# Narrow fp32 products of an RWKV-7 layer: one at a time, or four at a time in column groups

## The chip, the cores and the metric

The kernel runs on one core of one Trainium2 chip. The metric is the device time in microseconds of one execution. Times are the median of several executions; one further execution was taken with the hardware profiler, and all rows below come from that one.

## The reference

The program is a trunk of two layers over 512 frames of width 1024, batch 1. Layer 0 mixes time with RWKV-7, layer 1 with a convolution module; each is followed by cross-attention to 256 memory tokens and by a gated MLP. The change lies in the RWKV-7 mixer:

```
xr, xw, xk, xv, xa, xg = (h + xx * mu[i] for i in range(6))    # xx: the frame before, minus this one
r = xr @ w_r;  k = xk @ w_k;  v = xv @ w_v                      # 1024 x 1024 each
g = sigmoid(xg @ g1) @ g2                                       # g1: 1024 x 160
...
bonus = sum(rh * kh * r_k, axis=-1, keepdims=True) * vh         # one sum per head and frame, 16 heads of 64
out = ((y + bonus) * g) @ w_o
```

Two of its products have few output rows: the last 32 of the 160 columns of `g1`, and the bonus sums, of which there are 16 for each frame.

## The kernel before

Everything is held transposed, with features on the 128 partitions and the 512 frames in the free dimension, so the width of 1024 is 8 tiles of 128 x 512. TensorE multiplies a stationary block of weights (128 rows by up to 128 columns) with a moving tile of 128 x 512 and adds up in PSUM, over the 8 tiles. There are two kinds of product. The large ones split weights and activations into a high and a low part in the fp32r format and make three products of them (L181 to L183). The small ones take plain fp32 operands: the trace shows each of them as two matmul records and two weight loads.

*Gate stage* (`rwkv`, L388 to L400). For each of the 8 tiles, `mix(5, i, ...)` (L366) makes the mixed input on ScalarE and VectorE in one of eight `xh` buffers. A 128-column product with `g1a` (L393) and a 32-column product with `g1b` (L394, written to PSUM partitions 0 to 31) follow at once, so the two shapes alternate. Their sums go through a sigmoid (L399) and are parked in DRAM until the end of the mixer.

*k, r and v stages.* For each of the three, `mixes` (L402) makes 8 split inputs, and `gemm_cols` (L205) multiplies: output tiles 0 and 1 go side by side, one input tile after the other, then tiles 2 to 7, with `wsplit` splitting each block of weights. A callback takes each output tile: `k_done` (some 25 small operations on ScalarE and VectorE), `r_done`, `v_done`. `r_done(p)` (L574) makes one scratch tile `rk` and sums it over each head by a 16-column product (L585) that accumulates over all eight p in one PSUM tile held for the whole stage; after p = 7 the sums are split into rows 0 to 15 and 32 to 47 of `self.rows` (L587 to L590), which are read in the chain after v.

Between these products run substitution steps (`subst_a`, `subst_b`, called at fixed steps from L425). `subst_a(1)` starts after r tile 4: TensorE products (L609), then on VectorE a long chain of dependent operations (L618 to L633) that lasts through the start of the v stage.

The order on each engine is not written by hand here. A planner orders the instructions before the run, by priorities (mostly program order, some lowered by `lower`) and by its own estimate of when operands are ready. Each engine then works in that order and waits where an operand is late. Scratch tiles with the tag `tmp` rotate over six buffers (`NTMP`, L135), PSUM tiles over three `g`, three `h` and two `kv` banks (L139).

Of the kernel before, what the change touches and what calls it, by code (L numbers as in the profile page):

```python
# [11 lines left out]
ALU = mybir.AluOpType  # L12
# [5 lines left out]
KT = D // 128  # L18
NP = 8
# [91 lines left out]
class Builder:  # L111
# [212 lines left out]
    def rwkv(self):  # L324
        nc, a = self.nc, self.a
        with ExitStack() as cx:
# [27 lines left out]
            h = self.x  # L354
# [7 lines left out]
            for i in range(KT):  # L362
                nc.vector.scalar_tensor_tensor(out=h[:, i, :], in0=h[:, i, :], scalar=self.vec("g_mix0", i),
                                               in1=rs, op0=ALU.mult, op1=ALU.mult)

            def mix(m, i, tag="mf", bufs=2):  # L366
                mf = self.t(self.gp, [128, T], tag, bufs=bufs)
                nc.scalar.activation(mf, h[:, i, :], AF.Copy, scale=cpr[:, (5 + m) * KT + i : (5 + m) * KT + i + 1])
                nc.vector.scalar_tensor_tensor(out=mf[:, 1:], in0=h[:, i, : T - 1], scalar=self.vec(f"mu{m}", i),
                                               in1=mf[:, 1:], op0=ALU.mult, op1=ALU.add)  # L370
                return mf
# [3 lines left out]
            ps = self.ps()  # L375
            for i in range(KT):
                for m, w, o in ((1, w1, 0), (4, a1, 64)):
                    nc.tensor.matmul(ps[o : o + 64, :], w[:, i * 64 : (i + 1) * 64], mix(m, i, "xh", KT),
                                     start=i == 0, stop=i == KT - 1)
# [8 lines left out]
            g1a = self.wraw(a["g1a"], KT * 128)  # L388
            g1b = self.wraw(a["g1b"], KT * 32)
            ps, ps2 = self.ps(), self.ps()  # L390
            for i in range(KT):
                mf = mix(5, i, "xh", KT)
                nc.tensor.matmul(ps, g1a[:, i * 128 : (i + 1) * 128], mf, start=i == 0, stop=i == KT - 1)  # L393
                nc.tensor.matmul(ps2[:32, :], g1b[:, i * 32 : (i + 1) * 32], mf, start=i == 0, stop=i == KT - 1)  # L394
            self.gpark = self.t(self.dp, [160, T], "gpark")
            for r0, q in ((0, ps), (128, ps2[:32, :])):
                n = q.shape[0]
                sg = self.tmp()
                nc.scalar.activation(sg[:n], q, AF.Sigmoid)  # L399
                nc.sync.dma_start(self.gpark[r0 : r0 + n], sg[:n])  # L400
# [51 lines left out]
            for w, m, done in (("w_k", 2, k_done), ("w_r", 0, r_done),  # L452
                               ("w_v", 3, v_done)):
                srcs = [a[w][p] for p in range(NP)]
                lead = self.lead(srcs)
                self.gemm_cols(srcs, mixes(m), done, lead)
# [17 lines left out]
            for i in range(KT):  # L474
                nc.sync.dma_start(self.x[:, i, :], a["xT"][i])
            self.gemm_cols(wo, og, self.addx, lead)

    def rowbcast(self, half, p, s, tag):

        ps = self.ps(tag).rearrange("p (a t) -> p a t", a=2)  # L480
        for j in range(2):
            self.nc.tensor.matmul(ps[:, j], self.selb[half][:, (p + j) * 128 : (p + j + 1) * 128], self.rows[:, s],
                                  start=True, stop=True)
        return ps
# [89 lines left out]
    def r_done(self, p, psr):  # L574
        nc = self.nc
        r = self.AR[:, 1, p, :]
        rk = self.tmp()
        nc.vector.tensor_tensor(out=r, in0=psr, in1=r, op=ALU.mult)
        as3 = lambda x_: x_.rearrange("p (c t) -> p c t", t=C)
        for h in range(2):  # L580
            rows = slice(64 * h, 64 * h + 64)
            nc.vector.tensor_tensor(out=as3(rk)[rows], in0=as3(r)[rows], in1=self.bk[p][rows, :, 1 - h, :], op=ALU.mult)
        if p == 0:
            self.bonps = self.ps("h")
        nc.tensor.matmul(self.bonps[0:16, :], self.ws[:, p * 16 : (p + 1) * 16], rk, start=p == 0, stop=p == NP - 1)  # L585
        if p == NP - 1:
            b = self.rows = self.t(self.r1, [128, T], "zw", F32R)  # L587
            nc.vector.memset(b.bitcast(F32), 0.0)
            nc.scalar.copy(b[0:16], self.bonps[0:16, :])
            nc.vector.tensor_tensor(out=b[32:48], in0=self.bonps[0:16, :], in1=b[0:16], op=ALU.subtract)  # L590

    def bkt(self, p, h, c):
        return self.bk[p][64 * h : 64 * h + 64, c, :, :].rearrange("p b t -> p (b t)")
# [893 lines left out]
```

## Time and profile before

| what | value |
|---|---|
| time, median of 3 runs | 1658.86 us (1658.69 to 1660.44) |
| profiled execution, its own time | 1656.06 us |
| span in that execution, first to last instruction | 1654.3 us |
| TensorE matmul busy | 1613.1 us, 98% of the span |
| VectorE busy | 1106.0 us, 67% |
| ScalarE busy | 794.8 us, 48% |
| mean granted TensorE clock | 0.996 |

The profiled execution's time holds 1.8 us that lie outside the span. Busy shares are means over stages that differ; the rows further down look at the stages one by one. PE is TensorE, DVE VectorE, ACT ScalarE, and L394 is line 394 of the kernel.

### The profile page before, as it was taken

The page shows a single profiled execution, that of the slowest core. Times are in us where ns is not written, and L with a number is a line of the kernel's source. Part 1 is how long each engine was busy: PE and PEld are TensorE (multiplying, and loading weights), DVE is VectorE, ACT ScalarE, POOL GpSimd, SP SyncE. Part 2 cuts the span into 40 slices and gives each one's busy share as a digit, 9 for nine tenths or more (in the row PEclk, how much of TensorE's full clock was granted, in tenths as well). Part 3 has the DMA queues.
Part 4 walks back from the last instruction along what each step waited for, and adds up shares of the span by engine and source line. Part 5 has one row for each costly group of instructions (what it writes and reads, how often), then busy time and mean ns, then how long its engine had stood idle before and what let it go on. Part 6 is the DMA issues. An engine that isn't in the chain of part 4 may idle for free. (4 is left out here: it accounts for less than half of the span.)

```text
span 1654.3 us, 24232 instructions
## 1 busy us (share of the span) xinstructions
PE 1613.1 (98%) x9742; PEld 1293.5 (78%) x9742; DVE 1106.0 (67%) x1795; ACT 794.8 (48%) x1242; POOL 73.1 (4%) x101
## 2 busy tenths in 40 slices
PE   7999989899999999999999999999999999999998
PEld 6575558898888888888888777767888888888887
DVE  4779976568766667777732479877766677777323
ACT  5876635766454344434422366645533434444222
POOL 0000000000000000000000024430000000000000
PEclk9999999999999999999999999999999999999999
DMA  6333322103441233332333331223412333323332
GB/s 237 114 99 109 105 65 90 53 22 115 135 140 51 86 120 94 98 103 90 96 95 94 112 107 51 65 89 103 140 52 89 91 98 94 102 92 93 97 95 83
DMA packets 55151, 159.77 MB, mean 97 GB/s; under 512 B 6144, under 2 KB 10368, under 8 KB 55040
## 3 DMA queue, kind: packets, MB, share of 16 engines
q1 hardware_dynamic: 55040, 158.24, 30.8%
q8 instruction: 76, 1.25, 0.3%
q14 instruction: 35, 0.29, 0.1%
HBM read 150.55 MB, written 7.67 MB: 96 GB/s over the span
## 5 line engine op out<-in xcount | busy, mean ns | idle before, releaser
L176 ACT CAST wh<-raw 128x1024 fp32r<-128x1024 f32 (+1 forms) x227 | 235.1, 1037 | 503.4 <-PE g L182 396.2
L182 PE MATMUL g<-xl,wh 128*128 128x512 f32 x1152 | 451.0, 392 | 4.1 <-DVE xl L177 3.6
L181 PE MATMUL g<-xh,wh 128*128 128x512 f32 x1152 | 452.9, 394 | 0.7 <-ACT xh L176 0.7
L183 PE MATMUL g<-xh,wl 128*128 128x512 f32 x1152 | 451.0, 391 | 2.5 <-DVE wl L177 2.5
L177 DVE TENSOR_TENSOR wl<-raw,wh 128x1024 fp32r<-128x1024 f32 (+1 forms) x227 | 274.7, 1210 | 164.2 <-ACT wh L176 163.8
L182 PEld LDWEIGHTS g<-xl,wh 128*128 128x128 f32 x1152 | 216.9, 188 | 54.0 <-DVE xl L177 6.6
L183 PEld LDWEIGHTS g<-xh,wl 128*128 128x128 f32 x1152 | 216.9, 188 | 50.4 <-DVE wl L177 3.3
L181 PEld LDWEIGHTS g<-xh,wh 128*128 128x128 f32 x1152 | 216.9, 188 | 48.4 <-issue 1.8
L181 PE MATMUL g<-ah,wh 128*128 128x512 f32 (+1 forms) x374 | 141.0, 377 | 0.0
L183 PE MATMUL g<-ah,wl 128*128 128x512 f32 (+1 forms) x374 | 140.9, 377 | 0.0
L182 PE MATMUL g<-al,wh 128*128 128x512 f32 (+1 forms) x374 | 140.9, 377 | 0.0
L1157 DVE TENSOR_TENSOR z<-g,rs 128x512 f32<-128x512 f32 x88 | 60.4, 688 | 70.8 <-PE g L183 69.2
L181 PEld LDWEIGHTS g<-ah,wh 128*128 128x128 f32 x374 | 70.4, 188 | 13.0
L182 PEld LDWEIGHTS g<-al,wh 128*128 128x128 f32 x374 | 70.4, 188 | 12.9
L183 PEld LDWEIGHTS g<-ah,wl 128*128 128x128 f32 x374 | 70.4, 188 | 12.7
L1277 POOL TENSOR_TENSOR dg<-i,wsp 128x256 fp32r<-128x256 f32 x70 | 48.2, 721 | 657.3 <-DVE wsp L1231 573.0
L176 ACT CAST ah<-tmp 128x512 fp32r<-128x512 f32 x44 | 27.3, 622 | 100.9 <-DVE z L1156 95.8
L1299 DVE SCALAR_TENSOR_TENSOR h<-u,cdw,h 128x512 f32<-128x512 f32 x98 | 73.8, 753 | 2.3
L321 DVE TENSOR_TENSOR x<-x,g 128x512 f32<-128x512 f32 x39 | 26.8, 688 | 68.7 <-PE g L183 68.7
L1162 DVE SCALAR_TENSOR_TENSOR tmp<-z,fdw,tmp 128x512 f32<-128x512 f32 x88 | 66.0, 752 | 2.9
L1161 DVE SCALAR_TENSOR_TENSOR tmp<-z,fdw,tmp 128x512 f32<-128x512 f32 x88 | 65.5, 746 | 0.4 <-ACT tmp L1160 0.4
L1160 ACT ACTIVATE tmp<-z,fdw 128x512 f32<-128x512 f32 x88 | 63.2, 720 | 4.7 <-DVE z L1157 1.5
(351 smaller groups left out, 2445.4 us busy)
## 6 DMA issues: line engine op xcount, KB each, us to landing
raw<-wi SPq DMA_DIRECT2D x84, 512.0 KB, 3.5
raw<-wo SPq DMA_DIRECT2D x33, 512.0 KB, 3.5
raw<-wv SPq DMA_DIRECT2D x16, 512.0 KB, 3.6
raw<-cwi SPq DMA_DIRECT2D x14, 512.0 KB, 3.6
raw<-wq SPq DMA_DIRECT2D x12, 512.0 KB, 4.4
raw<-wxo SPq DMA_DIRECT2D x12, 512.0 KB, 3.5
raw<-wo SPq DMA_DIRECT2D x16, 384.0 KB, 3.1
raw<-wk SPq DMA_DIRECT2D x10, 512.0 KB, 3.8
```

Source lines behind the costliest of these rows:

```text
L176: self.nc.scalar.copy(h, src)
L177: self.nc.vector.tensor_tensor(out=l, in0=src, in1=h, op=ALU.subtract)
L181: mm(out, lh, rh, start=start, stop=False)
L182: mm(out, lh, rl, start=False, stop=False)
L183: mm(out, ll, rh, start=False, stop=stop)
L321: self.nc.vector.tensor_tensor(out=self.x[:, n, :], in0=self.x[:, n, :], in1=ps, op=ALU.add)
L1157: nc.vector.tensor_tensor(out=z[:, 2:], in0=ps, in1=rs(), op=ALU.mult)
L1160: nc.scalar.activation(y, z[:, 2:], AF.Copy, scale=cw(2))
L1161: nc.vector.scalar_tensor_tensor(out=y, in0=z[:, 1 : T + 1], scalar=cw(1), in1=y, op0=ALU.mult, op1=ALU.add)
L1162: nc.vector.scalar_tensor_tensor(out=y, in0=z[:, 0:T], scalar=cw(0), in1=y, op0=ALU.mult, op1=ALU.add)
L1277: nc.gpsimd.tensor_tensor(out=dg[:, h], in0=i2.unsqueeze(1).unsqueeze(1).to_broadcast([128, 2, 2, 64]), in1=wsp[:, :, i, h, 2 * g : 2 * g ...
L1299: nc.vector.scalar_tensor_tensor(out=ac, in0=u[:, jt : jt + T], scalar=cw(jt), in1=ac if n else ln["c"], op0=ALU.mult, op1=ALU.add if n el ...
```

## The change

In the gate stage the 32-column products wait until four mixed inputs are there. Then four of them are issued one after the other, each with its own block of weights, its own input and its own 32 partitions of one PSUM tile. This happens twice, and the second four accumulate on the first. The new `groupsum` then copies partitions 32 to 63 to a scratch tile on ScalarE and adds the other three quarters on VectorE.

For the bonus sums, `r_done` keeps the `rk` tiles of four steps. At p = 3 and p = 7 it issues four 16-column products into the four quarters of a fresh PSUM tile. The first tile goes through `groupsum` at p = 3, the four quarters of the second are added at p = 7, and then the sums are split as before.

```diff
             ps, ps2 = self.ps(), self.ps()
+            mfs = []
             for i in range(KT):
                 mf = mix(5, i, "xh", KT)
                 nc.tensor.matmul(ps, g1a[:, i * 128 : (i + 1) * 128], mf, start=i == 0, stop=i == KT - 1)
-                nc.tensor.matmul(ps2[:32, :], g1b[:, i * 32 : (i + 1) * 32], mf, start=i == 0, stop=i == KT - 1)
+                mfs.append(mf)
+                if i % 4 == 3:
+                    for j in range(4):
+                        k = i - 3 + j
+                        nc.tensor.matmul(ps2[32 * j : 32 * j + 32, :], g1b[:, k * 32 : (k + 1) * 32], mfs[k],
+                                         start=i == 3, stop=i == KT - 1)
...
-            for r0, q in ((0, ps), (128, ps2[:32, :])):
+            for r0, q in ((0, ps), (128, self.groupsum(ps2, 32))):
...
+    def groupsum(self, ps, rows):
+
+        nc = self.nc
+        s = self.tmp()[:rows]
+        nc.scalar.copy(s, ps[32 : 32 + rows])
+        for j in (0, 2, 3):
+            nc.vector.tensor_tensor(out=s, in0=ps[32 * j : 32 * j + rows], in1=s, op=ALU.add)
+        return s
...
-        if p == 0:
-            self.bonps = self.ps("h")
-        nc.tensor.matmul(self.bonps[0:16, :], self.ws[:, p * 16 : (p + 1) * 16], rk, start=p == 0, stop=p == NP - 1)
+        if p % 4 == 0:
+            self.rks = []
+        self.rks.append(rk)
+        if p % 4 == 3:
+            ps = self.ps("h")
+            for j in range(4):
+                k = p - 3 + j
+                nc.tensor.matmul(ps[32 * j : 32 * j + 16, :], self.ws[:, k * 16 : (k + 1) * 16], self.rks[j],
+                                 start=True, stop=True)
+            if p == 3:
+                self.brow = self.groupsum(ps, 16)
         if p == NP - 1:
+            s = self.brow
+            for j in range(4):
+                nc.vector.tensor_tensor(out=s, in0=ps[32 * j : 32 * j + 16], in1=s, op=ALU.add)
             b = self.rows = self.t(self.r1, [128, T], "zw", F32R)
             nc.vector.memset(b.bitcast(F32), 0.0)
-            nc.scalar.copy(b[0:16], self.bonps[0:16, :])
-            nc.vector.tensor_tensor(out=b[32:48], in0=self.bonps[0:16, :], in1=b[0:16], op=ALU.subtract)
+            nc.scalar.copy(b[0:16], s)
+            nc.vector.tensor_tensor(out=b[32:48], in0=s, in1=b[0:16], op=ALU.subtract)
```

## Rows read from the trace of the kernel before

**Rows 1.** The page's busy time by engine.
```profile
PE 1613.1 (98%) x9742; PEld 1293.5 (78%) x9742; DVE 1106.0 (67%) x1795; ACT 794.8 (48%) x1242; POOL 73.1 (4%) x101
```
**Rows 2.** Windows: stretch, length, busy and instructions per engine, PE clock, DMA share, GB/s.
```profile
47.98:64.12 16.14, 16.14 (x33) 3.37 (x31) 11.99 (x17) 13.89 (x21) 0.00 (x0) 1.00 0.38 130
64.12:75.16 11.04, 11.04 (x50) 9.12 (x50) 7.46 (x10) 7.21 (x13) 0.00 (x0) 1.00 0.58 174
...
206.00:224.20 18.20, 16.46 (x303) 11.67 (x303) 10.44 (x15) 5.00 (x10) 0.00 (x0) 1.00 0.20 60
224.20:256.80 32.60, 27.82 (x110) 18.99 (x109) 31.91 (x71) 13.54 (x19) 0.00 (x0) 1.00 0.23 67
```
**Rows 3.** Timeline of PE, gate stage: start, duration, line, tile, count [idle before].
```profile
50.96 1.04 PE L394 MATMUL g<-xh,raw 128*32 128x512 f32 x2
51.93 1.12 PE L393 MATMUL g<-xh,raw 128*128 128x512 f32 x2
```
**Rows 4.** Timeline of PE, one plain 128-column product among split products.
```profile
184.14 1.02 PE L1043 MATMUL kv<-raw,tt 128*128 128x512 f32 x2
184.76 0.63 PE L181 MATMUL g<-xh,wh 128*128 128x512 f32 x1
185.23 0.39 PE L182 MATMUL g<-xl,wh 128*128 128x512 f32 x1
```
**Rows 5.** Timeline of PE, one bonus product among split products.
```profile
208.28 0.39 PE L182 MATMUL g<-xl,wh 128*128 128x512 f32 x1
208.60 1.03 PE L585 MATMUL h<-tmp,wsc 128*16 128x512 f32 x2
209.56 0.50 PE L183 MATMUL g<-xh,wl 128*128 128x512 f32 x1
209.89 0.39 PE L181 MATMUL g<-xh,wh 128*128 128x512 f32 x1
```
**Rows 6.** Timeline of PE, two 64-column products in two column groups (L378).
```profile
39.88 1.08 PE L378 MATMUL g<-xh,raw 128*64 128x512 f32 x4
40.88 0.70 PE L987 MATMUL kv<-tt 128*128 128x256 f32 x2
```
**Rows 7.** Timeline of DVE, gate stage.
```profile
53.15 1.41 DVE L369 SCALAR_TENSOR_TENSOR xh<-x,vecs,xh 128x511 f32<-128x511 f32 x2
...
64.50 0.75 DVE L369 SCALAR_TENSOR_TENSOR mf<-x,vecs,mf 128x511 f32<-128x511 f32 x1 [2.38 <-ACT mf L368]
...
68.39 1.36 DVE L177 TENSOR_TENSOR xl<-mf,xh 128x512 fp32r<-128x512 f32 x2
```
**Rows 8.** Timeline of ACT, gate stage.
```profile
61.34 1.28 ACT L399 ACT_TABLE_LOAD   x1
63.26 0.60 ACT L399 ACTIVATE tmp<-g 128x512 f32<-128x512 f32 x1 [0.63 <-PE g L393]
```
**Rows 9.** Timeline of DVE, r stage and start of v.
```profile
212.16 0.69 DVE L578 TENSOR_TENSOR AR<-g,AR 128x512 f32<-128x512 f32 x1 [3.91 <-PE g L183]
...
244.23 0.68 DVE L590 TENSOR_TENSOR zw<-h,zw 16x512 fp32r<-16x512 f32 x1
...
256.13 0.69 DVE L177 TENSOR_TENSOR xl<-mf,xh 128x512 fp32r<-128x512 f32 x1
```
**Rows 10.** Waits in 198.8 to 256.9: engine, line, releaser: us, times, longest.
```profile
PE h L585 <- DVE tmp L582: 1.7, 3, 0.7
```
**Rows 11.** Timeline of PE, start of the v stage.
```profile
246.01 0.50 PE L182 MATMUL g<-xl,wh 128*128 128x512 f32 x1 [2.62 <-DVE xl L177]
```
**Rows 12.** Windows of PE alone: stretch, length, busy, clock, DMA share, GB/s.
```profile
239.70:252.30 12.60, 8.55 (x32) 1.00 0.17 48
252.30:256.80 4.50, 4.50 (x21) 1.00 0.45 120
190.30:192.80 2.50, 0.02 (x1) 0.50 0.55 198
192.80:197.20 4.40, 4.40 (x11) 0.51 0.69 205
```

## The prediction

> **What bounds the kernel now.** I read the page's busy times first: TensorE is busy 98% of the span [rows 1], so over the whole program a microsecond that it no longer needs is a microsecond gained, unless another engine feeds it too late at that place. So I then took windows around the two edits. In the gate stage TensorE is busy for all of 16.14 us, and for all of the 11.04 us after it, in which 48 split products for k tiles 0 and 1 run, 0.23 us each [rows 2]. VectorE and ScalarE have some slack there, 12.0 and 13.9 us of 16.1. From 206 to 224 VectorE is busy 10.4 us of 18.2, but from 224.2 to 256.8 it is busy 31.9 us of 32.6 while TensorE loses time [rows 2]: the end of the r stage and the start of v are bound by VectorE. The timelines and the waits then give prices.
>
> **Price of one narrow product.** A plain fp32 product of full width starts at 184.14 and the next instruction at 184.76; that one is followed after 0.47 us instead of 0.23. So the product takes 0.62 + 0.24 = 0.86 us [rows 4]. A bonus product takes 0.96 us to the next start, its successor 0.33 instead of 0.23, and its predecessor 0.32 instead of 0.23: 0.96 + 0.10 + 0.09 = 1.15 us [rows 5]. It is as long as a full one, though only 16 of 128 columns work, and changing the array's shape there and back costs 1.15 - 0.86 = 0.29 us. The gate stage agrees: 16.14 us / 8 = 2.02 us for a pair [rows 2], of which the 32-column one holds 0.97 [rows 3], and 2 x 0.86 + 0.29 = 2.01.
>
> **Price of a group of four.** The trace holds no four narrow products of this size at once. The nearest row has two: four records of L378, two products in two column groups with different inputs, start at 39.88, and the next instruction at 40.88 [rows 6]. Two take 1.00 us where one narrow product takes 0.97, so the second is nearly free. From below, four cost what one costs, 1.15 us; from above, one after the other, 4 x 0.86 + 0.29 = 3.73 us. I take 1.2 us, since the nearest row lies at the lower end. By the Trainium skill ("TensorE: Matmul & The Clock Gate", Part 3, measured speedup) four row tiles of 32 ran 3.07 times as fast as one after the other and three column tiles 2.38 times, not four and three times. By 3.07 a group would cost an estimated 3.44 / 3.07 + 0.29 = 1.41 us, and the four groups 0.8 us more in all; the pair in the trace points to less.
>
> **Gate stage.** TensorE: 8 x 0.86 + 2 x 1.2 = 9.3 us instead of 16.1, so 6.8 us less; it would be free at 57.3 instead of 64.12. The last two mixed inputs are there at 53.15 + 1.41 = 54.6 [rows 7]; tile 7 would be asked for at 55.2, so this just fits. But the next products need the split inputs of k, of which the last is finished at 68.39 + 1.36 = 69.75 [rows 7]. That chain does not hang on the narrow products, except that ScalarE, working in order, waits 0.63 us for TensorE before the sigmoid [rows 8], and VectorE then idles 2.38 us [rows 7]. The change takes the 0.63 away and adds a copy on ScalarE (0.60, by the sigmoid, which also reads PSUM [rows 8]) and three additions on VectorE (3 x 0.68 = 2.0, by the subtraction from PSUM on 16 partitions [rows 9]), which fit into that idle time. The second sigmoid waits for the additions, and the k inputs are queued behind it on ScalarE. So the last k input stays near 69.7, with bounds: 2.0 later if the additions fall on the path, 1.9 earlier if the planner moves table load and sigmoid forward by what TensorE gained. After it six products (1.4 us) remain: the pair of k tiles ends at 71.1 instead of 75.16. **Gain 4.1 us, between 2 and 5.9**; 6.8 is the ceiling set by TensorE. Inputs of tiles 0 to 3 keep their buffers until the first group, about 52.6; the k inputs that reuse them are made later than that, so holding them costs nothing. All work of `k_done` hangs on these k tiles and moves with them.
>
> **r stage.** TensorE: 8 x 1.15 + 1.7 of waits for `rk` [rows 10] = 10.9 us become 2 x 1.2 = 2.4, so 8.5 us less. How much of it arrives is VectorE's to say. Up to 212 VectorE waits for TensorE: 3.91 us before it can take r tile 4 [rows 9]. Four products less one group (4.6 - 1.2) bring that tile 3.4 us forward; the first group's additions (2.0) land in the shrunken idle time and delay it by up to 1.7. Behind it the fifth product and its wait fall away, so I let the substitution chain start 2.4 us earlier (1.7 to 3.5). From there VectorE is full, and four more additions after tile 7 (2.7 us) stand, by program order, before the inputs of v. I count 2.0 of them ahead of the last v input, finished at 256.82 [rows 9], which so comes 0.4 us earlier (0.8 earlier to 1.0 later, by 1.7 - 2.7 and 3.5 - 2.7; if the planner puts them all behind, 3.5 earlier). The rest comes from TensorE itself: it waited 2.62 us for v inputs at 246 [rows 11], and from 252.3 on was busy without a gap [rows 12], that is, behind. Of the 63 products on v inputs 0 to 6 (three output tiles, three products each) some 52 had run by 256.8 [rows 12]; the other 11 cost 2.5 us after the last input. With p = 5 to 7 thinned (3.45 + 1.0 of waits - 1.2 = 3.2 us) these are done before it. **Gain 0.4 + 2.5 = 2.9 us, between 0 and 6.** After that TensorE has v work ready and leads again.
>
> Holding `rk` tiles and a running sum takes up to five of the six scratch buffers; in the r stage only `r_done` takes new ones once the last `k_done` is through, so I price this at nothing; if `k_done` were short of them, VectorE's order would stretch by at most the time to the first group. The DMAs are the same in number and size.
>
> **Sum.** 4.1 + 2.9 = 7.0 us: the profiled execution's 1656.06 becomes 1649.1. The median of the runs shown lies 2.8 us above that execution, so 1658.86 - 7.0 = 1651.9, which is the forecast. Some 0.2%, 3.3 us, is what a measurement of this kernel can tell from no change.
>
> **Rivals.**
> *All of TensorE's saving arrives* (6.8 + 8.5 = 15.3 us: 1643.6). For it: 98% busy [rows 1]. Against: the full VectorE from 224 to 257 and the k inputs. Chance 0.10.
> *The additions and the feeding engines take it.* If the k inputs come 2.0 us later and the additions all stand before v, 2 + 0 to 1 us remain: about 1656.5, not to be told from before. For it: VectorE's 31.9 of 32.6 us [rows 2]. Chance 0.18. The Trainium skill ("TensorEngine Tiling (Array Packing)", PSUM Bottleneck) speaks for this case: packing speeds up TensorE but not the emptying of PSUM, which may become the limit.
> *The change does not do what it says:* the four products run one after the other. Then each group costs 3.73 us, TensorE saves 1.8 in each stage, and the additions take part of it: 1656 to 1659. The pair at 39.88 [rows 6] is against it. Chance 0.04.
> *Slower: the clock falls at the start of v.* From 190.3 to 192.8 TensorE did nothing, and from there to 197.2 the granted clock stood at 0.51, the lower level of 1.2 GHz, with 11 matmuls in 4.40 us, 0.40 us each instead of 0.23 [rows 12]. In the changed kernel TensorE is done with r earlier and waits longer than 2.62 us [rows 11] for v inputs; if the clock falls there and, since inputs trickle in, stays low, each matmul loses 0.17 us. It decides from 7.0 / 0.17 = 41 matmuls on. From 244 to 270 at half clock TensorE would do some 65 products instead of 113, 48 x 0.23 = 11 us lost; less the gain of 7.0 this is 4 us slower: 1663. Against it: after the 2.62 us wait of before the clock stayed at 1.00. Chance 0.11.
> The forecast has the rest, 0.57.
>
> **How the numbers follow.** The forecast's own range by the bounds above is 2 to 11.9 us of gain, 1647 to 1657. To leave out no more than 2 in 10, I extend it to 1644.5 below, most of the way to the first rival, and to 1659.5 above, over the two that end near no change. Faster by over 0.2% (below 1655.5): nearly all of the forecast's 0.57, the first rival's 0.10 and a little of the second, 0.71. Within 0.2%: 0.18. Slower: 0.11.
>
> **What would show it.** In the gate stage the eight records of four L394 products should start as two bunches of four, each group ending some 1.0 us after it began, and the split products of k should start near 57 to 58 and then wait for inputs. Starts 0.4 us apart within a group would show the third rival. In the r stage, two groups of L585, no idle ahead of tile 4 on VectorE, the four additions next to the substitution chain near 240, and a longer wait of TensorE before the third v input; a clock below 1.00 there is the fourth rival. The prediction is wrong if the planner's new order moves other work (weight splits, substitution steps, memory keys) into these waits or ahead of the inputs, which I can't read from this trace.

## The result, and the profile after

The changed kernel took 1666.8 us (median of 5, 1666.1 to 1667.9), the kernel before 1658.7 in the same comparison. The ratio is 1.0053, 95% interval 1.0041 to 1.0064: 6.8 to 10.6 us slower. Forecast were 1651.9 us and a range up to 1659.5. The forecast was wrong in sign.

The page's busy times: TensorE has 3.0 us more, where the forecast took 15.3 us of products away [rows 1]:

```profile
PE 1616.1 (97%) x9742; PEld 1298.7 (78%) x9742; DVE 1111.4 (67%) x1805; ACT 796.8 (48%) x1244; POOL 73.2 (4%) x101
```

These busy times do not measure work alone, since products last longer at a lower clock. In this execution the granted clock was 0.50 for 34.1 us (from 122.0 to 132.2, 197.0 to 210.7, 251.7 to 258.5 and 408.7 to 412.1 us), in the kernel before for 6.8 us (190.3 to 197.1).

The packing is not at fault. The timeline of TensorE (start, duration, line, tile, count) shows a group of four from 51.41 to 52.41, 1.00 us, where one narrow product took 0.97 [rows 3]. But the other groups were not left in one piece. After L399 (the old L394) the second gate group runs as one product and, 2.9 us later, three. Of the bonus products (L605, the old L585) only three run together:

```profile
51.41 1.07 PE L399 MATMUL g<-xh,raw 128*32 128x512 f32 x8
54.33 1.05 PE L399 MATMUL g<-xh,raw 128*32 128x512 f32 x2
57.22 1.06 PE L399 MATMUL g<-xh,raw 128*32 128x512 f32 x6
```

```profile
195.89 1.02 PE L605 MATMUL h<-tmp,wsc 128*16 128x512 f32 x2 [1.70 <-DVE tmp L597]
203.28 1.89 PE L605 MATMUL h<-tmp,wsc 128*16 128x512 f32 x2
207.49 1.89 PE L605 MATMUL h<-tmp,wsc 128*16 128x512 f32 x2
218.49 1.03 PE L605 MATMUL h<-tmp,wsc 128*16 128x512 f32 x2
243.36 1.05 PE L605 MATMUL h<-tmp,wsc 128*16 128x512 f32 x6
247.84 1.03 PE L605 MATMUL h<-tmp,wsc 128*16 128x512 f32 x2 [0.93 <-DVE tmp L597]
```

The program writes the four behind one another, but the planner, which goes by its own estimate of when operands are ready, has put other work between them. Two waits of TensorE have grown: one in `k_done` to 4.82 us (no wait there was over 1.2 us before), one at the third v input to 5.51 us (2.62 before, [rows 11]). Timeline of TensorE, what it waited for in brackets:

```profile
124.55 0.80 PE L536 MATMUL h<-cst,tmp 128*128 128x2 f32 x3 [4.82 <-ACT tmp L533]
255.04 1.22 PE L181 MATMUL g<-xh,wh 128*128 128x512 f32 x2 [5.51 <-ACT xh L176]
```

Each of them, and the 1.70 us wait at 195.89 too, stands beside a stretch in which the granted clock is 0.50, the level of 1.2 GHz. Windows of the changed kernel (the columns are those of [rows 2]):

```profile
124.60:132.20 7.60, 7.60 (x81) 6.20 (x82) 5.97 (x16) 3.92 (x8) 0.00 (x0) 0.50 0.06 19
198.90:210.70 11.80, 11.80 (x192) 6.53 (x194) 8.10 (x12) 6.22 (x9) 0.00 (x0) 0.50 0.28 90
255.00:258.50 3.50, 3.31 (x7) 2.12 (x8) 3.47 (x8) 1.49 (x3) 0.00 (x0) 0.50 0.00 0
```

And the inputs of r come later. Timeline of VectorE: the last three low halves of r inputs (L177) and the first r tile (L593, the old L578), first in the kernel before, then in the changed one:

```profile
169.84 0.68 DVE L177 TENSOR_TENSOR xl<-mf,xh 128x512 fp32r<-128x512 f32 x1
170.69 0.68 DVE L177 TENSOR_TENSOR xl<-mf,xh 128x512 fp32r<-128x512 f32 x1
173.76 0.68 DVE L177 TENSOR_TENSOR xl<-mf,xh 128x512 fp32r<-128x512 f32 x1
...
176.09 0.69 DVE L578 TENSOR_TENSOR AR<-g,AR 128x512 f32<-128x512 f32 x1
```

```profile
172.97 0.68 DVE L177 TENSOR_TENSOR xl<-mf,xh 128x512 fp32r<-128x512 f32 x1
...
184.77 0.68 DVE L177 TENSOR_TENSOR xl<-mf,xh 128x512 fp32r<-128x512 f32 x1
186.03 2.19 DVE L666 STREAM_TRANSPOSE c<-c 128x1024 f32<-128x1024 f32 x1
...
191.01 0.66 DVE L177 TENSOR_TENSOR xl<-mf,xh 128x512 fp32r<-128x512 f32 x1
192.49 0.69 DVE L593 TENSOR_TENSOR AR<-g,AR 128x512 f32<-128x512 f32 x1
```

The last input is 17 us late and the first r tile 16.4 us. The input now stands behind L666, a step that follows a substitution chain; in the kernel before the same step (L640) starts at 185.93, after the last input. Starts of the first product of a step, from TensorE's timeline, with the held kernels explained below:

| start, us | before | changed | order held | held, banks, late sums |
|---|---|---|---|---|
| k pair, input 1 | 64.12 | 58.20 | 57.42 | 56.74 |
| k pair, last input | 73.79 | 72.96 | 74.71 | 71.15 |
| k tile 7 | 124.89 | 126.28 | 125.82 | 122.24 |
| r pair, last input | 173.43 | 187.70 | 174.46 | 170.83 |
| r tile 7 | 232.05 | 237.83 | 228.65 | 224.98 |
| v, first input | 238.77 | 244.34 | 234.09 | 230.42 |
| v tile 7 | 285.32 | 296.19 | 287.68 | 279.53 |

So the changed kernel is 5.9 us ahead when k starts, 0.8 ahead at the end of the k pair, 1.4 behind at k tile 7, 5.8 behind at r tile 7 and 10.9 behind at v tile 7; after that the lag stays. The profiled execution of the kernel before was a fast one, 1656.06 us against a median of 1658.7, so the lag in these traces is larger than the measured 8.8 us (1.0053).

### The profile page after: what moved, and what is told of

It is laid out like the page before. It is cut to its first block, busy times and chain, and to the rows that moved or that the text cites. A ratio compares the mean times of both kernels' runs of the same rounds, so it can differ in the third digit from the quotient of the medians.

```text
span 1665.6 us, 24238 instructions
## 1 busy us (share of the span) xinstructions
PE 1616.1 (97%) x9742; PEld 1298.7 (78%) x9742; DVE 1111.4 (67%) x1805; ACT 796.8 (48%) x1244; POOL 73.2 (4%) x101
## 5 line engine op out<-in xcount | busy, mean ns | idle before, releaser
L181 PE MATMUL g<-xh,wh 128*128 128x512 f32 x1152 | 453.1, 395 | 6.6 <-ACT xh L176 5.7
L182 PE MATMUL g<-xl,wh 128*128 128x512 f32 x1152 | 452.6, 393 | 2.5 <-DVE xl L177 1.9
L183 PE MATMUL g<-xh,wl 128*128 128x512 f32 x1152 | 450.6, 391 | 0.1
L177 DVE TENSOR_TENSOR wl<-raw,wh 128x1024 fp32r<-128x1024 f32 (+1 forms) x227 | 274.5, 1210 | 164.0 <-ACT wh L176 163.4
L181 PEld LDWEIGHTS g<-xh,wh 128*128 128x128 f32 x1152 | 217.1, 189 | 56.7 <-ACT xh L176 7.7
L182 PEld LDWEIGHTS g<-xl,wh 128*128 128x128 f32 x1152 | 217.2, 189 | 52.4 <-DVE xl L177 4.8
L183 PEld LDWEIGHTS g<-xh,wl 128*128 128x128 f32 x1152 | 216.9, 188 | 45.7 <-DVE wl L177 0.6
L181 PE MATMUL g<-ah,wh 128*128 128x512 f32 (+1 forms) x374 | 140.9, 377 | 0.0
L182 PE MATMUL g<-al,wh 128*128 128x512 f32 (+1 forms) x374 | 140.8, 377 | 0.0
L183 PE MATMUL g<-ah,wl 128*128 128x512 f32 (+1 forms) x374 | 140.8, 377 | 0.0
L183 PEld LDWEIGHTS g<-ah,wl 128*128 128x128 f32 x374 | 70.4, 188 | 13.0
L182 PEld LDWEIGHTS g<-al,wh 128*128 128x128 f32 x374 | 70.4, 188 | 12.9
L181 PEld LDWEIGHTS g<-ah,wh 128*128 128x128 f32 x374 | 70.4, 188 | 12.8
```

The source lines that it names most:

```text
L177: self.nc.vector.tensor_tensor(out=l, in0=src, in1=h, op=ALU.subtract)
L181: mm(out, lh, rh, start=start, stop=False)
L182: mm(out, lh, rl, start=False, stop=False)
L183: mm(out, ll, rh, start=False, stop=stop)
```

## The experiments

Theories: **A**, the loss is the planner's new order; **B**, the feeding engines and the additions take what packing saves; **C**, the clock, which falls at TensorE's waits, gives it back. Ratios below are to the kernel before, run on the same chip (median 1657.2 to 1658.3 there); 0.001 is 1.7 us.

**Each part alone, the planner free.** The gate hunk or the bonus hunk of the change, the other left as before.

> Gate part of the change alone (32-column products in fours, their three additions), the planner free to order the work. Theory A (the loss comes from the planner's new order in the r stage): the gate part frees some 4 to 6 us in its own stage; whether they arrive depends on the order that the planner makes of it; if the r inputs stay where they were, 1653 to 1656. Theory B (the feeding engines take what packing saves): no change, 1658 to 1660. Theory C (packing lowers the clock): slower with longer half-clock stretches, 1660 to 1665.

> Bonus part alone (row sums in fours, four plus three additions), the planner free. Theory A: this part carries the loss if the r inputs are mixed later or the bonus products are placed apart, 1663 to 1668; if the order in the r stage stays, it gains 2 to 3 us, 1656. Theory B: 1658 to 1660 in either case. Theory C: as A in time, but with half-clock stretches before any wait for an input.

Gate alone 1665.65 us, ratio 1.0040 (1.0026 to 1.0054); bonus alone 1659.61, ratio 1.0010 (1.0001 to 1.0019). The miss is in the expectation of where the loss would sit: most of it, 6.6 of 8.8 us, comes with the gate hunk, though what is late is the r stage, 100 us further on. The gate hunk alone also has the 4.8 us wait in `k_done` and the late r inputs, so these do not come from the `rk` tiles that the bonus hunk holds. Bonus alone gains nothing, as B expected; it brings a wait of 5.21 us at a v input, where gate alone has 2.61.

**The same change in the order of before.** All engines' instructions are chained in the order that the planner made for the kernel before, without semaphores; the narrow products are taken out, and the groups of four stand at the places of the 4th and the 8th. `PLAN` has one list of program positions for each engine:

```diff
+        for e, s in PLAN.items():
...
+            for last, i in zip(order, order[1:]):
+                tc.add_manual_dep(i, last.name, mybir.DependencyInfo(mybir.DependencyClass.NoSync,
+                                                                     mybir.DependencyReason.DATA), reason="order")
```

> The whole change, but every engine's order held to that of the kernel before; only the narrow products are taken out and put back as groups of four side by side, with their copies and additions. Theory A (the new order is the cost): 1651 to 1655, 4 to 8 us faster than before. Theory B (additions and feeding engines take it): 1657 to 1660. Theory C (packing itself lowers the clock or runs in turn): 1660 or more.

> The gate part alone, every engine's order held to that of the kernel before. Theory A: the gate stage's own gain as forecast, 4.1 us (2 to 5.9), so 1653 to 1657. Theory B: 1658 to 1660. Against the run of the gate part with a free planner, the difference is what the planner's order does.

Both parts held: 1660.00, ratio 1.0009 (1.0000 to 1.0018). Gate alone held: 1658.75, ratio 1.0002 (0.9994 to 1.0011). So the new order costs 0.0044, some 7.3 us (5 to 10 by the two intervals), of the changed kernel's loss: theory A holds for the loss. But it doesn't hold for the forecast: with the order of before, packing gains nothing either. That is what B expected, but 1660.00 lies at the edge of B's range and of C's, so the time alone does not tell these two apart. The trace of the held kernel (the line numbers of these kernels are higher by the lists of orders, and differ by a few from one to the next: here L426 to L428 are the split products L181 to L183, L422 is L177, L645 L394, L653 the sigmoid L399, L639 L393, L863 the four additions, L867 and L868 the cast L589 and the subtraction L590) says why. Timelines of TensorE and ScalarE around the gate, TensorE first:

```profile
48.27 3.60 PE L639 MATMUL g<-xh,raw 128*128 128x512 f32 x8
...
56.42 1.06 PE L645 MATMUL g<-xh,raw 128*32 128x512 f32 x8
...
64.19 0.79 PE L426 MATMUL g<-xh,wh 128*128 128x512 f32 x1 [5.51 <-ACT tmp L653]
```

```profile
61.65 0.58 ACT L736 COPY tmp<-g 32x512 f32<-32x512 f32 x1
62.24 1.28 ACT L653 ACT_TABLE_LOAD   x1
63.54 0.60 ACT L653 ACTIVATE tmp<-g 128x512 f32<-128x512 f32 x1
```

TensorE waits for the sigmoid, not for k inputs: the second k tile takes the PSUM buffer that this sigmoid empties, since there are three buffers `g`, two of which the gate holds. And at the start of v, VectorE and ScalarE:

```profile
242.66 2.84 DVE L863 TENSOR_TENSOR tmp<-h,tmp 16x512 f32<-16x512 f32 x4
245.53 0.62 ACT L867 CAST zw<-tmp 16x512 fp32r<-16x512 f32 x1 [6.29 <-DVE tmp L863]
246.18 0.68 DVE L868 TENSOR_TENSOR zw<-tmp,zw 16x512 fp32r<-16x512 f32 x1 [0.68 <-ACT zw L867]
...
247.20 0.68 DVE L422 TENSOR_TENSOR xl<-mf,xh 128x512 fp32r<-128x512 f32 x1
247.94 0.80 PE L427 MATMUL g<-xl,wh 128*128 128x512 f32 x1 [6.00 <-DVE xl L422]
```

(the last row is TensorE's). All four additions, 2.84 us, then 0.68 us of idle for the cast, stand ahead of the third v input, so that TensorE goes on at 247.94 instead of 246.01 [rows 11], though VectorE had been 1.4 us ahead. The subtraction stands there in the kernel before too [rows 9]. The clock fell in both places; windows:

```profile
64.20:67.50 3.30, 3.30 (x8) 2.62 (x9) 2.51 (x5) 3.06 (x6) 0.00 (x0) 0.51 0.49 123
...
247.90:251.80 3.90, 3.86 (x8) 2.57 (x9) 3.90 (x9) 2.69 (x4) 0.00 (x0) 0.50 0.00 0
```

So three causes could hold the time: the buffer, the additions, the clock.

**The clock.** Products with weights of zero keep TensorE at work in its waits:

```diff
+    def warm(self, ps, n, at, alone=False):
+        zero = self.c("m32")[:, 0:1].to_broadcast([128, 128])
...
+            for _ in range(n):
+                self.nc.tensor.matmul(ps, zero, self.x[:, 0, :], start=alone, stop=alone)
```

> The packed kernel in the order of the kernel before (it took 1660.0), with eleven more products, with weights of zero, six in the 5.5 us in which TensorE waits from 58.7 us on and five in the 6.0 us from 241.9 on; nothing else is changed. Theory A2 (the clock: each of these waits is followed by 6.8 us at half clock, which costs up to 3.4 us): the half-clock stretches at 60.6 and 245.0 are gone and the time is 1653 to 1656. Theory B2 (the waits alone hold the time, the clock costs nothing): 1660, or 1 us more for the added work.

> The kernel before, its order held, with two products with weights of zero in TensorE's wait from 190.3 to 192.8 us, after which its clock was at half for 6.8 us. Theory A2: that stretch is gone and the time is 2 to 3.4 us less, 1655 to 1656.5. Theory B2: no change, 1658 to 1659.

> The changed kernel with its own order held (it took 1666.8) and fourteen products with weights of zero in four of its waits: five at 119.7, two at 194.2, two at 196.9, five at 249.5 us. Theory A2 (clock): half-clock stretches at 122, 197 and 251.7 us shrink or go, 10 to 17 us at half speed less, 1658 to 1662. Theory B2 (the order's waits alone): 1666 to 1668.

In the held kernel: 1660.33, ratio 1.0014 (1.0005 to 1.0023), no gain. In the gate stage the filling did its work, 17 products in 3.5 us at full clock instead of 8 in 3.3 us, and the work of k came 2.1 us earlier. Window:

```profile
64.00:67.50 3.50, 3.50 (x17) 2.88 (x16) 2.77 (x5) 3.12 (x6) 0.00 (x0) 1.00 0.63 165
```

But the third v input came at 247.96 as without it. That is the experiment's own fault: the products put in there delayed the second bonus group, and VectorE waited 2.10 us for it, as much as had been won. The half clock at 245 stayed too, and in all 20.4 us at 0.50 are left in that trace of 23.8 in the held kernel's. So this run does not say what the clock costs there.

In the kernel before, the time is 1657.25, ratio 0.9994 (0.9986 to 1.0003), no change. This run also shows that holding an order costs nothing that can be measured, since its order was held with the same lists. Windows of it: the wait at 190 is filled and at full clock, and the half clock, again 6.8 us, is at 246 instead, behind a wait at which the kernel before kept its clock [rows 12]:

```profile
189.90:192.50 2.60, 2.60 (x49) 1.26 (x42) 2.57 (x4) 2.56 (x5) 0.00 (x0) 1.00 0.79 297
242.30:244.90 2.60, 0.01 (x1) 0.01 (x1) 2.54 (x6) 0.57 (x1) 0.00 (x0) 1.00 0.51 117
245.80:252.60 6.80, 6.46 (x15) 4.30 (x14) 6.19 (x14) 4.14 (x6) 0.00 (x0) 0.50 0.01 1
```

In the changed kernel, in its own order, the filling gave 1663.82, ratio 1.0035 (1.0023 to 1.0048) against 1.0053, some 3 us, between the two expectations. The time at 0.50 fell from 34.1 to 10.2 us; the stretch from 199 to 211 is at full clock. Window:

```profile
198.90:210.70 11.80, 11.80 (x217) 8.10 (x217) 6.30 (x9) 4.42 (x7) 0.00 (x0) 1.00 0.27 92
```

So the clock is probably a part of what the new order costs, about 3 of 7.3 us; the intervals of the two ratios overlap, so the size is uncertain. What it costs the held kernel stays open.

**The PSUM buffer.** The gate part alone, held, with its two tiles among the buffers `h`, which are free then:

```diff
-            ps, ps2 = self.ps(), self.ps()
+            ps, ps2 = self.ps("h"), self.ps("h")
```

> The gate part alone in the order of the kernel before (it took 1658.75), with the gate's two PSUM tiles taken from the other group of banks, so that the second k tile need not wait for the first sigmoid. Theory A3 (that bank is what TensorE waits for from 57.7 to 63.2): products of k run from 57.7 on as their inputs come, the pair ends near 71 to 73 instead of 76, 1653 to 1656. Theory B3 (the k inputs are the limit in any case, and the bank only hides it): the pair ends no earlier than 75, 1658 to 1660.

1655.91, ratio 0.9986 (0.9977 to 0.9995), against 1.0002: 2.7 us. The 5.50 us wait is gone; TensorE now waits 2.12 us, for a k input (row of its timeline below, L427 is L181 there), and the last input of the pair starts at 71.24. The buffer was the limit, as A3 says.

```profile
64.89 0.51 PE L427 MATMUL g<-xh,wh 128*128 128x512 f32 x1 [2.12 <-ACT xh L422]
```

**The additions.** The last four go from their place ahead of the third v input (position 1733 of the program) behind the substitution chain, near 272 us (ahead of position 1946). The cast and the subtraction go with them, in the lists:

```diff
-            self.place(rest, DVE=(1733, "DVE"))
+            self.place(rest, DVE=(1946, "DVE"))
```

> The packed kernel in the order of the kernel before (1660.0), with the last four additions, the cast and the subtraction of the bonus sums moved on VectorE and ScalarE behind the substitution chain (near 272 us), where VectorE waits for 4.3 us. Theory A4 (these additions ahead of the third v input turn the r stage's lead of 1.4 us into a lag of 1.9 us): the third v input comes 3.4 us earlier, near 244, and the time is 1655.5 to 1657.5. Theory B4 (TensorE's own work after the v inputs sets the end): 1659 to 1661.

> The same with the gate's two PSUM tiles in the other group of banks as well. If the two gains add up (2.8 us by the banks, 3.4 by the later additions, from 1660.0): 1652.5 to 1655. If what the gate stage gains is lost again in a later wait or at half clock: 1656 to 1658.

> The same again with two products with weights of zero in each of two waits of TensorE, ahead of the fifth k input (62.8 us) and ahead of r tile 3 (near 188). If the clock is what these waits cost: 1 to 3 us less than without them and no half-clock stretch at 66 and 190 us. If not: the same time as without them, within 0.7.

Late sums alone: 1655.24, ratio 0.9989 (0.9980 to 0.9998) against 1.0009, 3.3 us, and TensorE goes on with the third v input at 244.10 instead of 247.94 (row below, L428 is L182 there). The trace has about as much time at 0.50 as the held kernel's, 20.4 of 23.8 us, so these 3.3 us are not the clock's in the main.

```profile
244.10 0.50 PE L428 MATMUL g<-xl,wh 128*128 128x512 f32 x1 [1.91 <-DVE xl L423]
```

With the buffers too: **1650.36, ratio 0.9964 (0.9952 to 0.9977), 6.0 us faster than before and the best of all.** The gains add up, 2.7 and 3.3 us alone and 7.5 together; the time is below what I expected. The time at 0.50 is down to 10.4 us there, so a part of the surplus may be the clock's, which no run separates. The busy times of its page, and TensorE's timeline at the third v input:

```profile
PE 1603.2 (97%) x9742; PEld 1292.2 (78%) x9742; DVE 1112.3 (67%) x1805; ACT 796.3 (48%) x1244; POOL 73.1 (4%) x101
```

```profile
240.23 0.50 PE L428 MATMUL g<-xl,wh 128*128 128x512 f32 x1 [1.91 <-DVE xl L423]
```

TensorE is 9.9 us less busy than before [rows 1], and 6.0 arrive. Not all of that is the packing's: the subtraction, which no longer stands ahead of the third v input, gives 0.7 us there and could have been moved in the kernel before too. Neither move was tried without packing.

Filling two more waits gave 1652.72, ratio 0.9971 (0.9961 to 0.9982): no gain. But the half clock went elsewhere: the stretch at 65.2 is gone, another came at 242.1 (windows below), where the kernel without filling kept 1.00, and in all there are 10.2 us at 0.50 as against 10.4. So this does not say what the clock is worth either.

```profile
65.20:68.70 3.50, 2.92 (x11) 1.90 (x11) 3.04 (x5) 3.06 (x6) 0.00 (x0) 1.00 0.64 216
242.10:245.50 3.40, 3.37 (x7) 2.27 (x8) 3.37 (x8) 1.84 (x3) 0.00 (x0) 0.50 0.00 0
```

**Which part of the new order.** The changed kernel, with only the feeding engines held, as in this diff against the fully held kernel (the lists stand as `...`), or only TensorE (`{"PE": ...}`):

```diff
-PLAN = {"PE": ..., "DVE": ..., "Activation": ..., "Pool": ..., "SP": ...}
+PLAN = {"DVE": ..., "Activation": ...}
```

> The changed kernel (1666.8) with the order of VectorE and ScalarE held to that of the kernel before, TensorE, GpSimd and SyncE as the planner orders them (products of memory keys early, the groups split). With all five orders held it took 1660.0. Theory A5 (the loss of 6.8 us between the two is the later place of the r inputs on VectorE and ScalarE): 1659 to 1662. Theory B5 (it is TensorE's own order, the split groups and the early memory keys): 1664 to 1668.

> The changed kernel with TensorE's order alone held to that of the kernel before, the groups in one piece; the other engines as the planner orders them. Theory A5: the r inputs may come late again, then 1663 to 1668; if holding TensorE also brings them back to their old place, 1658 to 1661. Theory B5: 1658 to 1662 in either case.

Feeders held: 1663.81, ratio 1.0035 (1.0022 to 1.0048). TensorE held: 1662.21, ratio 1.0025 (1.0016 to 1.0035). The first gives back 3.0 of the 7.3 us, the second 4.6; neither theory is right alone. With TensorE held, the planner puts the r inputs back in their places (the last input of the pair at 171.62), but then v inputs and the weights' low halves are late, and TensorE waits 4.16 and 2.47 us for them. With the feeders held, a wait of 3.39 us in `k_done` is left. Timelines of TensorE, first with TensorE held (L342 and L344 are L181 and L183), then with the feeders held (L614 is the L536 of above):

```profile
239.08 1.22 PE L342 MATMUL g<-xh,wh 128*128 128x512 f32 x2 [4.16 <-ACT xh L337]
...
255.43 0.70 PE L344 MATMUL g<-xh,wl 128*128 128x512 f32 x1 [2.47 <-DVE wl L338]
```

```profile
122.67 0.98 PE L614 MATMUL h<-cst,tmp 128*128 128x2 f32 x7 [3.39 <-ACT tmp L611]
```

Why the planner puts the r inputs where it does was not tried.

## Why the prediction was wrong

- *Price of a group, 1.2 us.* Right: 1.00 us from its start to the next instruction, and TensorE was done with the gate at 57.42 in the held kernel, forecast 57.3. The stage took 9.15 us from 48.27; less 8 x 0.86 for the full products this leaves 1.14 for a group. The third rival, four in turn, is out. By the Trainium skill's 3.07, which it gives for four row tiles ("TensorE: Matmul & The Clock Gate", Part 3, measured speedup), the estimate was 1.41; here four cost what one did.
- *The order otherwise unchanged.* This is the step that turned the sign. The sum moved its terms along the old order and put a new one at nothing; it named one only as what it could not read. The groups came apart, r inputs moved behind a substitution chain: 7.3 of the 15.8 us between forecast and result (7.0 faster forecast, 8.8 slower measured).
- *Gate, "that chain does not hang on the narrow products".* True of the chain of k inputs, but the products wait for something else first, the PSUM buffer. The forecast asked only which input comes last. Held, the k pair's last input came 0.9 us later than before instead of 4.1 earlier; with other buffers 2.6 earlier, inside the 2 to 5.9. The Trainium skill's sentence that packing leaves the emptying of PSUM as it was ("TensorEngine Tiling (Array Packing)", PSUM Bottleneck) bears on this wait, though it was one tile emptied late that cost 5.51 us here, not the speed of emptying; I had read it as a matter of the additions.
- *Three additions in VectorE's idle time.* Right: they ran from 62.33 to 64.45, and the 2.38 us of idle [rows 7] shrank to 0.34.
- *r stage, substitution 2.4 us earlier.* Right: in the held kernel r tile 4 is taken at 211.71 instead of 212.16 [rows 9], from a lag of 1.0 us at 207, and from 222 on VectorE is 1.4 ahead; 2.45 us.
- *"2.0 of them ahead of the last v input".* Mis-sized: all 2.84 us and 0.68 of idle stand ahead of the third v input already, so that a lead of 1.4 became a lag of 1.9, 3.4 us in all. Moved away together with the subtraction, they gave 3.3 us back. This is the second rival's mechanism, with a price of 3.4 instead of 2.
- *2.5 us of backlog after the v inputs.* In the best kernel the lead grows by 2.45 us in the r stage and by 0.7 at the start of v: 3.2 in all against 2.9 forecast. That the numbers are close is luck: the 0.7 is the subtraction moved away, and from there to v tile 7 the lead stays at 5.8, so no backlog was saved.
- *The clock as the slower rival.* It fell where the rival put it (255.0 to 258.5, 7 products in 3.5 us), and elsewhere, probably as about 3 us of what the new order costs. Filling waits in the kernels with held order gained nothing, but left about as much time at half clock, so its share there is open.

With order, buffer and additions put right, 6.0 of the forecast's 7.0 us are there. The sum is 7.3 + 3.3 + 4.1 (the buffers, from 0.9989 to 0.9964) + 1.0 (what is left) = 15.7; each of the first three is uncertain by 2 to 3 us and may hold a part that is the clock's.

## What to carry to other kernels

Where a planner orders the program, as here, a local change can be first of all a new order; hold the old order and change one thing, and the change's own worth can be read apart from it. Before time saved on one engine is booked, ask not only which input the next instruction needs, but which buffer it writes and who empties that. Additions that packing leaves behind can take back what it saves where they stand ahead of an awaited input; here they belonged where their engine was idle, not where the sums were complete.

## What the runs showed of the hardware

Four fp32 products of 32 columns on different column groups, with different moving inputs, took 1.00 us, one took 0.97 [rows 3]. A wait of 2.6 us did not always bring the lower clock: the kernel before kept 1.00 at 243 [rows 12], and when its wait at 190 was filled, 6.8 us at 0.50 came at 246 instead, with the same time. Likewise a wait of 1.91 us at 240: the best kernel kept 1.00 behind it, the same kernel with two other waits filled had 0.50 from 242.1 on. What decides between the two was not tried.
